# Expert gathers spread otherwise over the passes, modulation made during attention, and key norms by small matmuls, in a two-layer transformer kernel

## The chip, the cores and the metric

The kernel runs on one core of one Trainium2 chip. The metric is device time in microseconds, the median of several executions; less is better. Besides the median there is one profiled execution, and every duration quoted from the trace is from that one.

The core's engines each work through their own queue in order: PE (matmuls; PEld is its weight load), DVE (vector), ACT (activations and copies), POOL (general), and SP, which here only issues transfers. PE, ACT and POOL issue some transfers too.

## The reference, cut to what matters

Two layers run over 512 latent tokens and 256 context tokens of width 1024. Each layer does, for both kinds of token:

```python
# adaLN: six chunks of 1024 from silu(c) @ w_mod[l] + b_mod[l]; chunk 0 and 1 shift and scale the first norm,
# 2 gates the mixer's result, 3 and 4 shift and scale the second norm, 5 gates the experts' result
h = rms_norm(x, g) * (1 + scale) + shift
y = mixer(h)          # windowed attention, neighbourhood attention, RWKV-7, then one output projection
x = x + gate * y
h = rms_norm(x, g) * (1 + scale) + shift
x = x + gate * peer_ffn(h)

# in the RWKV-7 part, per head of 64 channels:
kk = kkh / maximum(sqrt(sum(kkh * kkh, axis=-1, keepdims=True)), 1e-12)

def peer_ffn(h, wq, sub_keys, u, v):      # 16384 experts, each one row of u and one of v
    s = scores of 8 heads against 2 x 128 sub-keys
    expert, best = 16 best of the sums, per head
    act = gelu(h . u[expert])
    return sum over the 128 chosen of softmax(best) * act * v[expert]
```

The context tokens leave no output of the last layer, so the second layer works out only the latent ones beyond its keys, values and states.

## The kernel before, in words

**Stages of a layer.** `project` makes the modulation and the norm, then the features of the RWKV part (`features`) and the queries, keys and values (`qkv`). `mix` runs the scan, the attention and the output projection. `peer` runs the norm, the scores, and the two dense passes over all experts, which the text calls U and V. In layer 0 the passes serve four tiles of 128 latent tokens, in layer 1 three.

**U pass.** 128 blocks of 128 experts. For each, a transfer brings two blocks' rows of `u` (1 MB), ACT casts `uH`, DVE makes the remainder `uL`, PE runs 8 x 3 matmuls into `pa`, and ACT writes `aw` (or the kept `ar`). Between blocks lie the pieces of the gates (`gates`): a piece spreads the 128 chosen gates of four tokens into a table over all experts, with two `oh` (L1231) and one `og` (L1234) of DVE, eight matmuls `pw` (L1239) and ACT's copy `W` (L1240). There are 128 pieces; after each eight `W`, which has one buffer, goes to memory (`wscr`, 2 MB). `GSPREAD` says over how many groups of four blocks the pieces are spread: 24 in layer 0. When the last piece is done, its pool is closed and a pool for later `ar` tiles (`late`) opens in the same memory; the first block that needs it is block 96.

**V pass.** The same 128 blocks, with `v` rows, `vH`, `vL`, the product `G` of gates and activations, its parts `GH` and `GL`, and 24 matmuls into `py` per block (18 in layer 1).

**Gathers.** The two context tiles (layer 0) and one latent tile (layer 1) take no dense pass. `class Gather` fetches for them the rows of `u` and `v` of one chosen expert per token with an indirect transfer of POOL (L1453, tile `row`, 128 tokens x 2048 numbers, 1.05 MB). Each pair of gathers then takes DVE two dot products (L1464), an activation, one multiply (L1467) and two multiply-adds (L1470). Layer 0 has 256 gathers, layer 1 has 128. They share their buffers `row` (`NROW` = 6) with the rows of `u` and `v`.

`NTICK` sets how many are issued: at each tick it adds a number to a balance, and each whole unit issues one gather at high priority. There is a tick at each of 5 steps of the scores, and after every second block: 24 in the first 12 groups of U, 40 in the rest of U, 64 in V. What is still left after V is issued by `flush()`. Then `ends` scales and adds the sums (L1399, L1400) and the `py` (L1409, L1410).

**Modulation.** `mod_unit` makes one chunk: 8 transfers of `wmod` (0.52 MB each), 32 matmuls, 4 of the bias, a copy `rmod`, two transfers out. In layer 0 chunks 0 and 1 stand ahead of the norm, and chunks 2 to 5 behind it at lower priority (`MOFF`). `mod_unit` is also called from `fill()`, which attention calls at places where PE may wait: there chunks 0 and 1 of layer 1 are made, in layer 0's context attention. Chunks 2 to 5 of layer 1 are made in layer 1's `project`.

**Key norms.** For each of four pairs of heads, a matmul with a block matrix of ones (`blk`, 128x128) sums the squares over 64 channels and repeats the sum in all of their rows: 128x768 numbers `rn`. ACT takes the root, DVE the maximum (L347) and the reciprocal (L348), POOL multiplies (L349). `rn` shares its buffer with ACT's `sg` (L360), by the tag "sg".

Order within an engine's queue comes from a scheduler that follows the written order and the priorities.

Of the kernel before, what the change touches and what calls it, by code (L numbers as in the profile page):

```python
# [8 lines left out]
F32 = mybir.dt.float32  # L9
# [4 lines left out]
AF = mybir.ActivationFunctionType  # L14
OP = mybir.AluOpType
AX = mybir.AxisListType
PSUM = bass.MemoryType.PSUM

P = 128
D = 1024  # L20
KC = 8
T = 768
NLAT = 512
NCTX = 256
NT = 6
# [9 lines left out]
LATER = 2000  # L35
NROW = 6
NQ = 2
MOFF = 500
GSPREAD = (24, 20)
LATE = (28, 28)  # L40
NM1 = 2
NMW = (6, 4)
NRAW = 4
TC0 = 6
NPSC, NPSL = 2, 4
# [9 lines left out]
NPRT = 4  # L55
NQKB = {"qs": 3, "kh": 3, "kl": 2}

NTICK = ((1, 1.0, 1.5, 2.4), (0, 0, 1.06, 1.06))
NFIRST = (12, 3)
FEATS = (12, 13, 4, 0, 5, 1, 6, 2, 7, 3, 14, 8, 9, 10, 11)  # L60
LAT = (0, 1, 2, 3)
# [5 lines left out]
class Kernel:  # L67
    nw = 0

    def __init__(self, ctx, tc, i, out, dbg):  # L70
        self.ctx, self.tc, self.nc, self.i, self.out, self.dbg = ctx, tc, tc.nc, i, out, dbg
        self.cp = ctx.enter_context(self.pool(name="cp", bufs=1))
        self.mods = list(range(NM1))

        self.xsb = {}
        self.consts()
        self.scratch()
# [150 lines left out]
    def project(self, l, st):  # L228
        tc, nc, i = self.tc, self.nc, self.i
        wc = l == 0  # L230
        cpl = self.colp[l]
        hp_ = st.enter_context(self.pool(name="hp", bufs=1))
        hH = hp_.tile([P, KC, T], F32R, name="hH")
        hL = hp_.tile([P, KC, T], F32R, name="hL")
        def mods(chunks):
            if s3.pools is None:
                s3.pools = [s3.enter_context(self.pool(name="mp", bufs=NMW[l], side="right")),
                            s3.enter_context(self.pool(name="mps", bufs=2, space=PSUM, side="right"))]
            self.mod(l, chunks, *s3.pools)

        def src(t):
            if l == 0:
                return i["x"][t * P:(t + 1) * P] if t < 4 else i["ctx"][(t - 4) * P:(t - 3) * P]
            return self.xp[t * P:(t + 1) * P]
        with ExitStack() as s3:
            s3.pools = None
            if l == 0:
                mods(range(2))
            with ExitStack() as s2:
                np_ = s2.enter_context(self.pool(name="np", bufs=2))  # L250
                nps = s2.enter_context(self.pool(name="nps", bufs=2, space=PSUM))
                mc = self.mcol[:, l, 0]
                for tiles in (CTX, LAT[:2], LAT[2:]):
                    self.norm_T(src, mc, hH, hL, tiles, np_, nps)
            if l:
                self.gat.close()
            with self.tc.high_priority(offset=-MOFF):
                mods(range(NM1 if l else 2, 6))
        ps = st.enter_context(self.pool(name="pps", bufs=2, space=PSUM))
        psn = st.enter_context(self.pool(name="psn", bufs=2, space=PSUM, side="right"))  # L260
        xp_ = st.enter_context(self.pool(name="xp", bufs=1, side="right"))
        win = i["w_in"][l].rearrange("(k p) n -> p k n", p=P)
        pre = st.enter_context(self.pool(name="pre", bufs=1)).tile([P, KC, 256], F32, name="pre")
        with ExitStack() as s2:
            b2 = s2.enter_context(self.pool(name="b2", bufs=2))
            pb = s2.enter_context(self.pool(name="pb", bufs=1))
            with self.tc.high_priority(offset=PREO):
                nc.sync.dma_start(pre, win[:, :, QKV0:QKV0 + 256])
            last = self.features(l, s2, win, hH, hL, ps, psn, xp_, b2, pb)
        with ExitStack() as s2:  # L270
            self.qkv(l, s2, win, hH, hL, ps, psn, pre)
        last()
# [9 lines left out]
    def features(self, l, st, win, hH, hL, ps, psn, xp_, b2, pb):  # L282

        nc, i = self.nc, self.i
        wc = l == 0
# [3 lines left out]
        gn = 6 if wc else 4  # L289
# [43 lines left out]
        for h in range(4):  # L333
# [4 lines left out]
            kk = b2.tile([P, T], F32, name="kk")  # L338
            nc.vector.tensor_scalar(kk, kf, cpl[:, KKC + h:KKC + h + 1], None, OP.mult)
            sq = b2.tile([P, T], F32, name="sq")  # L340
            nc.scalar.activation(sq, kk, AF.Square)
            rn = pb.tile([P, T], F32, name="rn", tag="sg")
            for (o, m) in segs:
                pz = ps.tile([P, m], F32, name="pf", tag=f"pf{m}")
                nc.tensor.matmul(pz, self.blk, sq[:, o:o + m], start=True, stop=True)
                nc.scalar.activation(rn[:, o:o + m], pz, AF.Sqrt)
            nc.vector.tensor_scalar(rn, rn, 1e-12, None, OP.max)  # L347
            nc.vector.reciprocal(rn, rn)  # L348
            nc.gpsimd.tensor_tensor(kk, kk, rn, OP.mult)  # L349
            nc.sync.dma_start(self.fm[2, :, h], kk)  # L350

            kAB, rate = [], []
            for d in range(2):
                sg = pb.tile([P, T], F32, name="sg", tag="sg")
                sga = b2.tile([P, T], F32, name="sga")
                r = slice(d * 64, d * 64 + 64)
                for (o, m) in segs:
                    pz = ps.tile([P, m], F32, name="pf", tag=f"pf{m}")
                    nc.tensor.matmul(pz, w2[r, h * P:(h + 1) * P], th[r, o:o + m], start=True, stop=True)
                    nc.scalar.activation(sg[:, o:o + m], pz, AF.Sigmoid, bias=cpl[:, W0 + 4 * d + h:W0 + 4 * d + h + 1])  # L360
                    pz = ps.tile([P, m], F32, name="pf", tag=f"pf{m}")
# [5 lines left out]
                for z in range(2):  # L367
# [4 lines left out]
                    c = b2.tile([P, NG, 65], F32, name="pr")  # L372
# [23 lines left out]
                                 bias=ka2[:, h:h + 1])  # L396
            nc.gpsimd.tensor_tensor(pd[:, :n], pd[:, :n], kf[:, :n], OP.mult)
            nc.gpsimd.tensor_tensor(pd[:, :n], pd[:, :n], rf[:, :n], OP.mult)
            pbn = psn.tile([P, gn, 2], F32, name="pn")
            for t in range(gn):  # L400
                nc.tensor.matmul(pbn[:, t], pd[:, t * P:(t + 1) * P], rkb[:, h], start=True, stop=True)
            nc.vector.tensor_copy(bon[:, :gn, 2 * h:2 * h + 2], pbn)
# [25 lines left out]
    def ngram(self, h, kAB, nmask, xp_, psn):  # L428


        nc = self.nc
        Nm = xp_.tile([P, 2, NG, 64], F32, name="Nm", bufs=2)
        for e in range(2):
            s = slice(e * 64, e * 64 + 64)
            for c0 in (0, 6):
                pn = psn.tile([P, 6, 64], F32, name="pn")
                for c in range(6):
                    for d in range(2):
                        nc.tensor.matmul(pn[64 * d:64 * d + 64, c], kAB[d][1][s, c0 + c], kAB[d][0][s, c0 + c],
                                         start=True, stop=True)  # L440
                nc.vector.tensor_tensor(Nm[:, e, c0:c0 + 6], pn, nmask.unsqueeze(1).to_broadcast([P, 6, 64]), OP.mult)
        for d in range(2):
            for j in range(2):
                r = 64 * d + 32 * j
                nc.sync.dma_start(self.nscr[h, d, j].rearrange("q s t -> s q t"),
                                  Nm[r:r + 32, :, :, 32 * j:32 * j + 32].rearrange("s e c t -> s (e c) t"))

        Nt = xp_.tile([112, 32, 32], F32, name="Nt", bufs=2)
        X = xp_.tile([112, 32, 32], F32, name="X", bufs=2)
        nc.sync.dma_start(Nt[0:48], self.nscr[h, 0].rearrange("j q s t -> (j q) s t"))  # L450
        nc.sync.dma_start(Nt[48:64], self.nscr[h, 0, 0, 0:16])
        nc.sync.dma_start(X[64:112], self.nscr[h, 1].rearrange("j q s t -> (j q) s t"))
        return Nm, Nt, X
# [110 lines left out]
    def attention(self, l, st):  # L564

        nc, i = self.nc, self.i
        wc = l == 0
        ap = st.enter_context(self.pool(name="ap", bufs=1))
        a2 = st.enter_context(self.pool(name="a2", bufs=2))
        psl = st.enter_context(self.pool(name="psl", bufs=NPSL, space=PSUM))  # L570
# [4 lines left out]
        mp = st.enter_context(self.pool(name="mp", bufs=2))  # L575

        def fill():
            if self.mods:
                self.mod_unit(1, self.mods.pop(0), mp, psl, "pl")

        def soft(parts, h, use_sink):

# [97 lines left out]
        if wc:  # L680
            heads_A(CTX, False)
            for c in range(2):
                o = a2.tile([P, NLAT], F32, name="o")[:, :NCTX]
                qs = [load_q(3 + c, z, NLAT, T) for z in range(2)]
                hd = [load_k(5 + c, z, NLAT) for z in range(2)]
                for a in range(2):
                    prTs = []
                    for z in range(2):
                        pl = psl.tile([P, 512], F32, name="pl")
# [15 lines left out]
        for c in range(2):  # L705
            o = a2.tile([P, NLAT], F32, name="o")
            qs = [load_q(3 + c, z, 0, NLAT) for z in range(2)]
            hd = [load_k(5 + c, z, 0) for z in range(2)]
            for j in range(4):
                prTs = []  # L710
                for z in range(2):
# [4 lines left out]
                    pl = psl.tile([P, 512], F32, name="pl")  # L716
# [704 lines left out]
class Gather:  # L1421
# [51 lines left out]
    def tick(self, z):  # L1473
        self.due += NTICK[self.l][z]
        while self.due >= 1 and self.todo:
            self.due -= 1
            with self.K.tc.high_priority(offset=100000):
                self.gather(*self.todo.pop(0))
# [75 lines left out]
```

## Time and the profile before

| | |
|---|---|
| median of 3 runs | 5100.41 us (5096.14 to 5110.7) |
| profiled execution | 5089.21 us, its span 5087.4 us |
| mean granted clock of PE | 0.906 of full speed |
| PE busy | 4438.3 us (87%) |
| DVE busy | 3738.1 us (73%) |
| ACT / POOL busy | 1731.5 us / 1338.2 us |
| moved by transfers | 1186.55 MB, mean 233 GB/s |

Of layer 0, modulation and norm take 0 to 73 us, features to 372, queries to 518, the scan to about 726, attention and output projections with the context's scores and choice to 1048, norm and scores to 1125, U to 2064, V to 2838, what follows V to 2885. Layer 1 starts there: norm to 2919, features to 3180, queries to 3346, scan, attention and output projection to 3692, scores to 3811, U to 4517, V to the end at 5087.

The rows below are read so: the busy time of an engine in a stretch says how near it is to being the bound there; the idle time before an instruction, in brackets, names what ended it; `x` is a count of instructions (a matmul of the modulation counts twice, so a chunk has 72).

### The profile page before, as it was taken

To read this page: it belongs to the slowest core of one execution; us is meant where nothing else is said; L and a number is where in the kernel's file an instruction comes from. 1 tells how busy PE (TensorE), PEld (TensorE's weight loads), DVE (VectorE), ACT (ScalarE), POOL (GpSimd) and SP (SyncE) were. 2 spreads that over 40 slices of the span, in tenths; PEclk is the share of its full clock that TensorE was granted. 3 is DMA by queue.
4 is the path that set the end of the run, shared out by engine and by line. 5 is a ranking of instruction groups with operands and counts; after the bars stand their busy time and mean duration, and the time that the engine had idled before them with its cause. 6 is when DMAs were issued, how large, how long until landed. Compare 5 with 4: busy or idle time off the path is not lost. (4 is left out here: it accounts for less than half of the span.)

```text
span 5087.4 us, 74067 instructions
## 1 busy us (share of the span) xinstructions
PE 4438.3 (87%) x27525; PEld 3679.1 (72%) x27525; DVE 3738.1 (73%) x7611; ACT 1731.5 (34%) x2881; POOL 1338.2 (26%) x1403
## 2 busy tenths in 40 slices
PE   7778797689999979898889596799698998988999
PEld 4558666567888867787777364687578997977887
DVE  3964658869967754798888867758589877556887
ACT  3433234333333322222222244324333443332333
POOL 0536632011111111232222235455011111112121
PEclk9779887799999989999999787779799998999999
DMA  7434665235777755899999942573424887567998
GB/s 273 134 104 125 190 203 177 90 128 197 250 260 283 281 217 214 305 372 371 367 364 368 349 162 87 131 204 111 157 100 170 305 296 278 215 236 256 342 357 299
DMA packets 573865, 1186.55 MB, mean 233 GB/s; under 512 B 63152, under 2 KB 376384, under 8 KB 520768
## 3 DMA queue, kind: packets, MB, share of 16 engines
q1 hardware_dynamic: 507072, 758.39, 44.8%
q0 software_dynamic: 61440, 418.41, 22.1%
q10 hardware_dynamic: 4992, 5.02, 0.3%
q8 instruction: 216, 3.54, 0.3%
q14 instruction: 145, 1.19, 0.1%
HBM read 1005.19 MB, written 176.50 MB: 232 GB/s over the span
## 5 line engine op out<-in xcount | busy, mean ns | idle before, releaser
L1453 POOL DMA_INDIRECT row<-in_uv,eidx x384 | 580.2, 1511 | 2465.2 <-DVE accc L1470 1369.1
L136 PE MATMUL pa<-hH,uL 128*128 128x512 f32 (+1 forms) x2048 | 757.9, 370 | 36.0 <-DVE uL L1313 35.9
L134 PE MATMUL pa<-hH,uH 128*128 128x512 f32 (+1 forms) x2048 | 754.5, 368 | 25.8 <-ACT ar L1317 21.6
L135 PE MATMUL pa<-hL,uH 128*128 128x512 f32 (+1 forms) x2048 | 752.4, 367 | 0.0
L135 PE MATMUL py<-vL,GH 128*128 128x512 f32 x1792 | 705.9, 394 | 26.6 <-DVE vL L1365 26.5
L136 PE MATMUL py<-vH,GL 128*128 128x512 f32 x1792 | 698.4, 391 | 0.0
L134 PE MATMUL py<-vH,GH 128*128 128x512 f32 x1792 | 625.2, 397 | 67.5 <-ACT vH L1363 44.1
L1464 DVE SCALAR_TENSOR_TENSOR row<-row,h2c 128x1024 f32<-128x1024 f32 x384 | 467.6, 1220 | 293.6 <-DMA row<-in_uv,eidx 293.3
L1470 DVE SCALAR_TENSOR_TENSOR accc<-row,dt,accc 128x1024 f32<-128x1024 f32 x384 | 491.6, 1280 | 5.4
L1311 ACT CAST uH<-row 128x1024 fp32r<-128x1024 f32 x256 | 268.5, 1050 | 653.7 <-PE pa L135 582.2
L136 PEld LDWEIGHTS pa<-hH,uL 128*128 128x128 f32 x2048 | 391.4, 191 | 84.8 <-DVE uL L1313 45.8
L134 PEld LDWEIGHTS py<-vH,GH 128*128 128x128 f32 x1792 | 340.9, 191 | 148.6 <-ACT vH L1363 53.4
L134 PEld LDWEIGHTS pa<-hH,uH 128*128 128x128 f32 x2048 | 391.6, 191 | 66.6 <-ACT ar L1317 22.2
L135 PEld LDWEIGHTS pa<-hL,uH 128*128 128x128 f32 x2048 | 390.9, 191 | 39.4
L135 PEld LDWEIGHTS py<-vL,GH 128*128 128x128 f32 x1792 | 341.3, 190 | 105.6 <-DVE vL L1365 34.5
L1313 DVE TENSOR_TENSOR uL<-row,uH 128x1024 fp32r<-128x1024 f32 x256 | 311.8, 1220 | 128.4 <-ACT uH L1311 127.5
L136 PEld LDWEIGHTS py<-vH,GL 128*128 128x128 f32 x1792 | 339.6, 189 | 70.7
L1370 ACT CAST GH<-G 128x512 fp32r<-128x512 f32 (+1 forms) x256 | 145.0, 567 | 637.7 <-PE py L135 414.9
L1365 DVE TENSOR_TENSOR vL<-row,vH 128x1024 fp32r<-128x1024 f32 x256 | 309.4, 1218 | 26.5 <-ACT vH L1363 26.5
L1363 ACT CAST vH<-row 128x1024 fp32r<-128x1024 f32 x256 | 262.5, 1043 | 41.7 <-DMA row<-in_uv 23.1
L1239 PE MATMUL pw<-og,oh 128*128 128x128 f16 x1792 | 237.7, 297 | 33.5 <-DVE og L1234 23.5
L1231 DVE TENSOR_TENSOR oh<-iota,ix 128x512 f16<-128x512 f16 x448 | 170.5, 419 | 104.8 <-PE pw L1239 103.9
(385 smaller groups left out, 8577.1 us busy)
## 6 DMA issues: line engine op xcount, KB each, us to landing
row<-in_uT SPq DMA_DIRECT2D x128, 1024.0 KB
row<-in_uv SPq DMA_DIRECT2D x128, 1024.0 KB
wscr<-W SPq DMA_DIRECT2D x28, 2048.0 KB
wmod<-in_w_mod SPq DMA_DIRECT2D x96, 512.0 KB
wt<-wscr SPq DMA_DIRECT2D x32, 1024.0 KB
row<-in_wq SPq DMA_DIRECT2D x24, 1024.0 KB
ascr<-aw SPq DMA_DIRECT2D x96, 256.0 KB
av<-ascr SPq DMA_DIRECT2D x48, 512.0 KB
```

The lines of the kernel that those rows point to most:

```text
L134: mm(out, lh, rh, start=first, stop=False)
L135: mm(out, lh, rl, start=False, stop=False)
L136: mm(out, ll, rh, start=False, stop=last)
L1231: nc.vector.tensor_tensor(oh[:, z], self.iota4, ix[:, z, tt].unsqueeze(1).to_broadcast([P, P, 4]), OP.is_equal)
L1239: nc.tensor.matmul(pw[:, q], oh[:, 1, :, q], og[:, z, :, q], start=z == 0, stop=z == 1)
L1311: nc.scalar.copy(uH, ur)
L1313: nc.vector.tensor_tensor(uL, ur, uH.bitcast(F32), OP.subtract)
L1363: nc.scalar.copy(vH, vr)
L1365: nc.vector.tensor_tensor(vL, vr, vH.bitcast(F32), OP.subtract)
L1453: self.K.nc.gpsimd.indirect_dma_start(out=r, out_offset=None, in_=self.K.i[f"uv{self.l}"], in_offset=bass.IndirectOffsetOnAxis(ap=self.idx ...
L1464: nc.vector.scalar_tensor_tensor(rows[z][:, 0:D], rows[z][:, 0:D], 1.0, self.h[:, a], OP.mult, OP.mult, accum_out=dt[:, z:z + 1])
L1470: nc.vector.scalar_tensor_tensor(acc, v, dt[:, z:z + 1], acc, OP.mult, OP.add)
```

## The change

**The table of ticks.** `NTICK` goes in layer 0 from 1 gather per tick in the scores, 1.0 in U's first 12 groups, 1.5 in the rest and 2.4 in V to 2, 1.8, 2.1 and 1.9; in layer 1 from 1.06 in U and V to 1.2 in U and 1.0 in V. Counted on DVE's queue, layer 0 had 88 gathers added up in the scores and U, 151 in V and 17 behind V; now it has 142, 114 and none.

**The modulation.** Only chunks 0 and 1 of layer 0 are made in `project`. Chunks 2 to 5 of layer 0 come in the first four fills of layer 0's attention, then all six of layer 1 in every third fill (`NMA`). The buffers for `wmod` in attention are two, as before there; in `project` of layer 0 there were six.

**The key norms.** Six small matmuls put the sums with tokens on partitions (128x12 for a pair of heads), where root, maximum and reciprocal are taken; twelve matmuls against the identity spread them back over the 64 channels into `pf`, and DVE multiplies from there in place of POOL. `rn` has its own buffer.

```diff
-MOFF = 500
-NM1 = 2
-NMW = (6, 4)
+NMA = 3
...
-NTICK = ((1, 1.0, 1.5, 2.4), (0, 0, 1.06, 1.06))
+NTICK = ((2, 1.8, 2.1, 1.9), (0, 0, 1.2, 1.0))
...
-        self.mods = list(range(NM1))
+        self.mods = [(0, c) for c in range(2, 6)] + [(1, c) for c in range(6)]
+        self.fills = 0
...
-            s3.pools = None
-            if l == 0:
-                mods(range(2))
+            if wc:
+                self.mod(l, range(2), s3.enter_context(self.pool(name="mp", bufs=6, side="right")),
+                         s3.enter_context(self.pool(name="mps", bufs=2, space=PSUM, side="right")))
...
-            with self.tc.high_priority(offset=-MOFF):
-                mods(range(NM1 if l else 2, 6))
...
-            rn = pb.tile([P, T], F32, name="rn", tag="sg")
+            pz = psn.tile([P, NT, 2], F32, name="pn", tag="pn")
+            for t in range(NT):
+                nc.tensor.matmul(pz[:, t], sq[:, t * P:(t + 1) * P], self.blk[:, 0::64], start=True, stop=True)
+            rn = b2.tile([P, NT, 2], F32, name="rn")
+            nc.scalar.activation(rn, pz, AF.Sqrt)
+            nc.vector.tensor_scalar(rn, rn, 1e-12, None, OP.max)
+            nc.vector.reciprocal(rn, rn)
             for (o, m) in segs:
                 pz = ps.tile([P, m], F32, name="pf", tag=f"pf{m}")
-                nc.tensor.matmul(pz, self.blk, sq[:, o:o + m], start=True, stop=True)
-                nc.scalar.activation(rn[:, o:o + m], pz, AF.Sqrt)
-            nc.vector.tensor_scalar(rn, rn, 1e-12, None, OP.max)
-            nc.vector.reciprocal(rn, rn)
-            nc.gpsimd.tensor_tensor(kk, kk, rn, OP.mult)
+                for a in range(0, m, P):
+                    for e in range(2):
+                        nc.tensor.matmul(pz[64 * e:64 * e + 64, a:a + P],
+                                         rn[:, (o + a) // P, e:e + 1].to_broadcast([P, 64]),
+                                         self.ident, start=True, stop=True)
+                nc.vector.tensor_tensor(kk[:, o:o + m], kk[:, o:o + m], pz, OP.mult)
...
         def fill():
-            if self.mods:
-                self.mod_unit(1, self.mods.pop(0), mp, psl, "pl")
+            self.fills += 1
+            if self.mods and (self.mods[0][0] == 0 or self.fills % NMA == 0):
+                self.mod_unit(*self.mods.pop(0), mp, psl, "pl")
```

In the rows of the changed kernel, line numbers before the attention are lower by up to nine, and those of U, V and the gathers are the same.

**ACT at the close of the gates in layer 0's U pass.** The rows are the queue of ACT between the last block that goes to memory and the first block of the `late` pool (`ar`). `W` is a piece of the gates, `dt` one pair of gathers, `uH` a block's cast. Before:

```order
L1240 ACTIVATE W<-pw 128x128x4 x2
L1311 CAST uH<-row 128x1024
L1240 ACTIVATE W<-pw 128x128x4 x4
L1466 ACTIVATE dt<-dt 128x2
L1240 ACTIVATE W<-pw 128x128x4 x9
L1466 ACTIVATE dt<-dt 128x2
L1240 ACTIVATE W<-pw 128x128x4
L1317 ACTIVATE ar_17363<-pa 128x512
```

The same place now, from the last block that goes to memory:

```order
L1466 ACTIVATE dt<-dt 128x2
L1240 ACTIVATE W<-pw 128x128x4 x5
L1466 ACTIVATE dt<-dt 128x2
L1240 ACTIVATE W<-pw 128x128x4 x2
L1466 ACTIVATE dt<-dt 128x2
L1240 ACTIVATE W<-pw 128x128x4 x6
L1466 ACTIVATE dt<-dt 128x2
L1240 ACTIVATE W<-pw 128x128x4 x3
L1466 ACTIVATE dt<-dt 128x2
L1240 ACTIVATE W<-pw 128x128x4 x16
L1317 ACTIVATE ar_17886<-pa 128x512
```

From the last `aw` on, 16 pieces stood there before and 34 stand there now (two of these, ahead of the rows, beside a `uH`), and five pairs of gathers stand in the rows in place of two.

**SP at the end of layer 0's context attention.** The rows are transfers that SP issues in order: `wmod` and `bmod` of the modulation, `qs`, `kh` and `kl` of the attention, `gr` the gate of the context's output projection, for which chunk 2 must be made, `TT` and `UV` of the scan. Before:

```order
L164 DMA wmod<-in_w_mod 128x1024 x4
L830 DMA TT_4536<-tscr 64x512 x2
L831 DMA UV_4538<-vt 64x512 x2
L628 DMA qs<-qkT 64x256 x4
L628 DMA kl<-qkT 64x256
L628 DMA kh<-qkT 64x256 x2
L628 DMA qs<-qkT 64x256
L622 DMA oT<-o 128x256
```

The same place now:

```order
L163 DMA wmod<-in_w_mod 128x1024 x6
L156 DMA bmod<-in_b_mod 4x256
L628 DMA kh<-qkT 64x256
L163 DMA wmod<-in_w_mod 128x1024 x2
L628 DMA qs<-qkT 64x256 x2
L628 DMA kl<-qkT 64x256
L628 DMA kh<-qkT 64x256
L163 DMA wmod<-in_w_mod 128x1024
L622 DMA oT<-o 128x256
L1057 DMA row<-od 128x512
L1068 DMA gr<-mscr 128x1024
L163 DMA wmod<-in_w_mod 128x1024 x5
```

Before, the `wmod` of the attention ended ahead of the loads of the context's second half; now they go on between them, eight more follow the five, and in all the queue has 80 of them in the attention where it had 16.

**DVE at the first pair of heads of layer 0.** `rn` are the norms, `kk` the keys, `raw` and `mcol` what stands between. Before:

```order
L347 TENSOR_SCALAR rn<-rn 128x768
L304 SCALAR_TENSOR_TENSOR raw<-pf,colp_71,raw 128x255
L348 RECIPROCAL rn<-rn 128x768
L339 TENSOR_SCALAR kk<-raw,colp_71 128x768
L179 COPY mcol<-pm 128x2x8
```

And now:

```order
L339 TENSOR_SCALAR rn<-rn 128x12
L295 SCALAR_TENSOR_TENSOR raw<-pf,colp_71,raw 128x255
L340 RECIPROCAL rn<-rn 128x12
L330 TENSOR_SCALAR kk<-raw,colp_71 128x768
L348 TENSOR_TENSOR kk<-kk,pf 128x512
L348 TENSOR_TENSOR kk<-kk,pf 128x256
```

Maximum and reciprocal run over 12 columns in place of 768, and two multiplies of 512 and 256 columns have come to DVE.

## Rows read from the trace of the kernel before

**Rows 1.** Busy time by stretch: us, then each engine, PE's clock, DMA share, GB/s.

```profile
0.00:73.00 73.00, 43.19 (x359) 14.32 (x359) 24.57 (x74) 26.92 (x51) 2.06 (x11) 0.88 0.99 356
100.00:160.00 60.00, 57.63 (x396) 38.97 (x395) 42.94 (x41) 30.84 (x42) 26.69 (x17) 0.97 0.55 194
180.00:280.00 100.00, 67.49 (x388) 49.77 (x386) 98.98 (x148) 41.37 (x56) 48.63 (x31) 0.72 0.29 95
634.00:995.00 361.00, 286.82 (x2487) 226.21 (x2487) 274.12 (x934) 143.76 (x318) 87.50 (x122) 0.80 0.49 154
1123.00:1370.00 247.00, 239.81 (x1131) 196.38 (x1130) 236.55 (x869) 88.56 (x128) 43.01 (x66) 0.99 0.59 205
1370.00:1812.00 442.00, 442.00 (x2313) 366.45 (x2313) 319.79 (x531) 158.10 (x250) 63.40 (x46) 1.00 0.76 278
1832.00:1874.00 42.00, 14.33 (x108) 11.31 (x105) 26.38 (x51) 8.87 (x17) 4.57 (x3) 0.54 0.62 233
2064.00:2838.00 774.00, 716.89 (x3070) 582.31 (x3071) 673.16 (x913) 211.77 (x328) 228.85 (x154) 0.98 0.99 361
2838.00:2885.00 47.00, 0.71 (x7) 0.28 (x9) 45.28 (x64) 1.64 (x7) 13.42 (x8) 0.54 0.91 343
2885.00:2919.00 34.00, 24.27 (x176) 9.18 (x176) 21.71 (x58) 22.89 (x46) 2.45 (x3) 0.70 1.00 358
4518.00:5087.00 569.00, 533.21 (x2304) 437.39 (x2304) 439.91 (x622) 191.81 (x288) 99.82 (x63) 0.97 0.89 310
```

**Rows 2.** PE's instructions one by one around the end of layer 0's V pass.

```profile
2836.68 0.39 PE L135 MATMUL py<-vL,GH 128*128 128x512 f32 x1
...
2838.26 0.39 PE L136 MATMUL py<-vH,GL 128*128 128x512 f32 x1
2884.94 1.08 PE L161 MATMUL pm<-wmod,cs 128*32 128x256 f32 x8 [46.29 <-DMA wmod<-in_w_mod]
```

**Rows 3.** Waits in V of layer 0 (2100 to 2826 us): total, times, longest.

```profile
PEld py L134 <- ACT vH L1363: 53.4, 22, 5.7
```

**Rows 4.** DVE's groups in U and V of layer 0, shapes apart.

```profile
L1470 DVE SCALAR_TENSOR_TENSOR accc<-row,dt,accc 128x1024 f32<-128x1024 f32 x239 | 306.0, 1280 | 3.5
L1464 DVE SCALAR_TENSOR_TENSOR row<-row,h2c 128x1024 f32<-128x1024 f32 x239 | 290.7, 1220 | 136.9 <-DMA row<-in_uv,eidx 136.6
L1231 DVE TENSOR_TENSOR oh<-iota,ix 128x512 f16<-128x512 f16 x256 | 97.6, 419 | 65.0 <-PE pw L1239 64.6 <-issue 0.2
L1234 DVE TENSOR_TENSOR og<-oh,g 128x1024 f16<-128x1024 f16 x128 | 86.0, 683 | 0.0
```

**Rows 5.** DVE's groups behind layer 0's V pass (2838 to 2885 us).

```profile
L1410 DVE TENSOR_TENSOR row<-row,yt 128x512 f32<-128x512 f32 x8 | 5.1, 681 | 0.0
```

**Rows 6.** ACT's first kept tile of the late pool, and the idle time ahead.

```profile
1874.04 1.09 ACT L1317 ACTIVATE ar<-pa 128x512 f32<-128x512 f32 x2 [12.76 <-DMA wscr<-W]
```

**Rows 7.** PE's work on the modulation (L161) by stretch.

```profile
0.00:73.00 73.00, 32.61 (x304) 8.17 (x304) 0.88 0.99 356
100.00:160.00 60.00, 10.46 (x128) 3.50 (x128) 0.97 0.55 194
634.00:726.00 92.00, 12.95 (x144) 3.18 (x144) 0.96 0.58 174
2919.00:3020.00 101.00, 15.36 (x160) 4.30 (x160) 0.89 0.57 193
```

**Rows 8.** Groups on ACT and DVE in layer 0's features (73 to 372 us).

```profile
L360 ACT ACTIVATE sg<-pf,colp 128x512 f32<-128x512 f32 x8 | 5.5, 686 | 20.7 <-POOL kk L349 20.6
L348 DVE RECIPROCAL rn<-rn 128x768 f32<-128x768 f32 x4 | 19.8, 4939 | 0.0
```

**Rows 9.** SP's queue one by one in layer 0's context attention.

```profile
663.00 7.80 SPq L164 DMA_DIRECT2D wmod<-in_w_mod  x2
680.89 6.94 SPq L164 DMA_DIRECT2D wmod<-in_w_mod  x4
```

**Rows 10.** Waits in the first part of layer 1's V pass (4518 to 4720 us).

```profile
DVE row L1464 <- DMA row<-in_uv,eidx: 55.8, 13, 9.5
```

More of the change, by code (lines that the diff above doesn't have):

```diff
@@ L234, in project @@
         hL = hp_.tile([P, KC, T], F32R, name="hL")
[L235 to L239, printed above, removed]
         def src(t):
@@ L398, in features @@
             nc.gpsimd.tensor_tensor(pd[:, :n], pd[:, :n], rf[:, :n], OP.mult)
-            pbn = psn.tile([P, gn, 2], F32, name="pn")
+            pbn = psn.tile([P, gn, 2], F32, name="pn", tag="pn")
             for t in range(gn):
@@ L435, in ngram @@
             for c0 in (0, 6):
-                pn = psn.tile([P, 6, 64], F32, name="pn")
+                pn = psn.tile([P, 6, 64], F32, name="pn", tag="pn")
                 for c in range(6):
```

## The prediction

> **What bounds the kernel now.** I read the busy times by stretch first, since the bound changes from stage to stage [rows 1]. At the start the transfers are the limit: DMA share 0.99 from 0 to 73 us. The features pass between PE (57.63 of 60 us from 100 on) and DVE (98.98 of 100 from 180 on, at a granted clock of 0.72). In attention and what surrounds it (634 to 995) no engine is full: PE 286.82 and DVE 274.12 of 361. The early part of U is held by two engines at once, DVE 236.55 and PE 239.81 of 247; its middle by PE alone (442 of 442, DVE 319.79). V of layer 0 is the odd stage: PE 716.89, DVE 673.16 of 774, and DMA share 0.99 at 361 GB/s.
>
> How far V is from PE's own limit comes from the instructions at its end: seven steps from 2836.68 to 2838.26 us, so 0.226 us per matmul [rows 2]. 24 x 128 matmuls make 3072 x 0.227 = 697 us. V took 774, so 77 us are lost, and the waits name late rows of `v`: 53.4 us of PE's weight loads stood for `vH` [rows 3]. Behind V, PE is idle for 46.29 us, until the next layer's `wmod` [rows 2], while DVE adds up the last gathers (45.28 of 47 us busy) [rows 1].
>
> The profiled execution took 5089.2 us, 11 less than the median; the sum is made against it, and 11 us are put on at the end. About 0.3%, 15 us, is what a measurement of this kernel can tell from no change.
>
> **Start and features of layer 0: -32 us.** In the first 73 us PE counts 304 matmul records of modulation [rows 7]; chunks 0 and 1 are 144, so 160 (2.2 chunks of 8 x 0.52 MB, 9.3 MB) are of chunks that now go elsewhere. At 356 GB/s these are 26 us. Bounds -4 and -18: the weights and tokens still have to come, and the norm behind `mcol` remains; I take -12. From 100 to 160, where PE is full, 10.46 us of PE's time go [rows 1, 7]; I take -8. Key norms: four reciprocals of 4.94 us on DVE [rows 8] and their maxima go; in their place come two multiplies per pair of heads. Those read PSUM as the sums behind V do, 0.68 us for 512 columns [rows 5], about 1.1 together, so some 4 us less per pair, 17 in all, part of it where DVE is full. ACT's `sg` also waited 20.7 us for POOL's `kk`, only because they share a buffer [rows 8]; that wait goes, but the matmul that feeds `sg` may be late next. The twelve new matmuls per pair are small and lie where PE has 30 of 100 us free [rows 1]. Between 0 and -50, near the DVE time in the full stretch: -12.
>
> **Attention of layer 0: +25 us.** 64 tiles of `wmod` come in. 144 records (16 tiles) took PE 12.95 us [rows 7], so 64 cost about 52 us. PE has 74 us idle in 634 to 995 [rows 1], but part of that is time in which DVE works on the choice and PE has nothing to be mixed with. If all fits, 0; if nothing fits, 52. SP's queue is the second cost: two buffers mean that it stands until PE has used a tile. Four tiles took 6.94 us, two took 7.80 [rows 9], 1.7 to 3.9 each. In SP's order 13 tiles now stand together at the end of the context's part, ahead of the latent `qs` and `kh` (23 us at 1.74 each), and chunk 2 is needed for `gr` of the context's projection. Taken as half of PE's 52; bounds 0 and +60.
>
> **Scores and U of layer 0: +48 us.** 54 more gathers are added up there. One costs DVE 1.22 + 1.28 = 2.50 us [rows 4], and I take 2.66 with the two short instructions that go with these. In the first 12 groups the ticks give 19 more (24 x 0.8), 51 us of DVE, where DVE has 10 us left [rows 1]. So the pieces of the gates slide: 18 more (16 to 34) stand in the bunch before the late pool. A piece takes DVE 2 x 0.419 + 0.683 = 1.52 us [rows 4], so 27 us leave the early part, and 51 - 27 - 10 = 14 remain, say +15. The bunch: 16 pieces kept PE from dense work for 42 us (busy 14.33) [rows 1], ended by `W` going out, ACT waiting 12.76 us [rows 6]. Without that wait a piece costs (43 - 13) / 16 = 1.9 us, with it 2.7; 18 more and 2 to 4 more gathers are +38 to +58, I take 50. In that stretch 108 matmuls, 8 to a piece, took PE 14.33 us [rows 1], about 1 us a piece, so PE has some 17 us less among the blocks before. So +33 there. The other 35 gathers fall where DVE has 122 of 442 us free [rows 1] and cost nothing; without that cover they would be 93 us. Bounds +15 and +80.
>
> **V of layer 0: -38 us.** 37 gathers fewer of 1.05 MB each. 774 us at 361 GB/s are 279 MB; 240 remain, 665 us, below PE's 697. So PE bounds, and the gain is at most 77. Layer 1's V is the model for what stays: 18 x 128 x 0.227 = 523 us of matmuls took 561 in all at DMA share 0.89 [rows 1], a loss of 38. Left with such a loss, V takes 736. Bounds 0 and -77.
>
> A rule stands beside this. The Trainium skill, "DMA: Bandwidth & Descriptors", section Bandwidth, gives 425 GB/s as measured for a 16 MB transfer, and warns there that HBM to SBUF is bound near 358 GB/s per core. By the first figure V's 279 MB would need 657 us (an estimate), PE would bound already and V would gain nothing; the row shows 361 GB/s at a share of 0.99, so the trace agrees with the second.
>
> **Behind V: -34 us.** No gather is left for the flush. What remains is `ends`: eight sums at 0.68 us for `py` [rows 5], the products ahead of them alike, about 11 us. 46.3 becomes 12. Bounds -25 and -38.
>
> **Project of layer 1: -31 us.** Chunks 2 to 5 no longer share the transfers from 2885 to 2919 (share 1.00) [rows 1], -9; 15.36 us of PE's modulation leave the next 101 us [rows 7], which PE bounds as in layer 0, -10; key norms as in layer 0, -12. Bounds 0 and -65.
>
> **Gathers of layer 1: -3 us, 15 either way.** Nine gathers go from V to U; early V waits 55.8 us on DVE for gathers [rows 10], which one gather per tick in place of 1.06 changes little.
>
> The sum: -32 + 25 + 48 - 38 - 34 - 31 - 3 = -65. 5089 - 65 = 5024 profiled, 5035 as a median.
>
> **The rivals.**
>
> *U hides its gathers.* DVE's 10 free us in the early part are a total of busy time; if the pieces' slide costs what it frees (PE's 17 us among the blocks, and the bunch overlapping the casts for the next blocks), U comes out at 0 instead of +48: -113, a median of 4987. For it speaks that PE and DVE are idle in the bunch for two thirds and a third of the time; against it that the bunch is serial through the one buffer of `W`.
>
> *V is not shortened.* V's loss may come from the sharing of six `row` buffers, not from bytes: each gather holds a buffer until DVE is through, and U will now hold them likewise. Then V keeps its 774, the rest stands: -65 + 38 = -27, and with U at its upper half (+63), -12: a median of 5088. For it speaks that `vH` waits for few long gaps (22 waits, 5.7 at most) [rows 3]; against it the share of 0.99 over the whole stage.
>
> *SP and PE are held by the modulation in attention: slower.* A fill's matmuls stand in PE's queue, and everything behind them waits for their tile. At 3.75 us per tile (the slow row) [rows 9], 64 tiles are 240 us; less the 74 us of idle PE [rows 1] that is +166 in place of +25: +76, a median of 5176. It decides from about +105 us in that stage, where the other terms (-90) are used up and 15 remain. For it speaks that PE stands in order and the buffers are two; against it that tiles back to back took 1.74 us and that the scheduler puts other matmuls between most of them.
>
> That the change doesn't do what it says is excluded for the gathers and the chunks by the counts in the queues. It is open only for the price.
>
> **How the numbers follow.** The forecast, with its sum between -30 and -95, has 0.55; U hiding its gathers 0.17; V not shortened 0.16; the slower rival 0.12. Predicted is 5035. Of the forecast about 0.04 lies within 15 us of 5100; of V not shortened about half. Faster by over 0.3%: 0.51 + 0.17 + 0.09 = 0.77; within: 0.04 + 0.07 + 0.01 = 0.12; slower: 0.11. The range 4970 to 5105 holds the forecast, most of the first rival and most of the second; the slower one lies outside, as does a U that hides everything with V at PE's limit. The forecast's own range is 5005 to 5070.
>
> **What the profile after would show.** Right: V of layer 0 near 736 us with DMA share clearly under 0.99; PE idle behind V about 12 us; no more than 0.5 us for any reciprocal of the key norms and no `sg` waiting for `kk`; PE's gap before the late pool between 80 and 100 us; the first feature matmul near 61 us in place of 73. Wrong: a gap before the late pool of 45 us or below (first rival); V at 760 or more (second); from scan's end to the context's choice longer by over 100 us with PE waiting on `wmod` (third). The prediction would also fail if the late context path (chunks 2 to 4) delayed the choice of experts, so that gathers are missing at U's first ticks and pile up again behind V.

## The result, and the profile after

The changed kernel takes 5242.09 us (median of 4 runs, 5238.32 to 5246.49) where the kernel before takes 5101.0 (median of 4). The ratio is 1.0274, interval 1.0257 to 1.0292: slower by 141 us where 65 us less were forecast. The forecast's range ended at 5105. The profiled execution has a span of 5244.7 us at a granted clock of 0.889, against 5087.4 at 0.906, so the two traces differ by 157 us. Differences below are between medians measured side by side, unless a ratio is named.

Where these 157 us arise is read from the start of the first or last matmul of a stage in both traces; U and V are taken from DVE's first `uL` and `vL`, and attention ends with its last score matmul:

| stage | before, us | after, less before | forecast |
|---|---|---|---|
| start to first feature matmul, layer 0 | 73.0 | -4 | -12 |
| features and queries, to the scan's first matmul | 448.3 | +22 | -20 |
| scan to its last matmul | 203.5 | +25 | in attention |
| from there to the end of attention | 239.2 | +140 | +25 |
| output projection, norm and scores | 161.3 | +3 | in U |
| U with the step to V | 938.5 | +42 | +48 |
| V | 774.6 | -28 | -38 |
| behind V, to layer 1's first feature matmul | 80.8 | -45 | -43 |
| layer 1, from there to U | 823.1 | -8 | -22 |
| U and V of layer 1 | 1336.9 | +9 | -3 |

Some 10 us of the scan are probably chance of the one profiled execution of before, which was 11 us under its median: in all the runs below, also where its code is the same, the scan takes 5 to 25 us more.

Busy times by stretch after, columns as in [rows 1]: the start, the attention with the context's scores and choice, a piece of it, U's early part, its middle, V, and what lies behind V.

```profile
0.00:69.00 69.00, 35.65 (x196) 11.77 (x196) 23.79 (x71) 26.37 (x48) 3.38 (x12) 1.00 0.61 215
661.00:1102.00 441.00, 338.38 (x2914) 232.39 (x2913) 255.02 (x842) 116.31 (x256) 88.60 (x125) 0.73 0.64 201
780.00:800.00 20.00, 8.39 (x64) 1.61 (x64) 0.00 (x0) 0.37 (x1) 0.00 (x0) 0.50 0.68 202
1312.00:1545.00 233.00, 220.22 (x995) 177.80 (x995) 223.97 (x783) 74.47 (x112) 60.65 (x75) 0.99 0.71 245
1545.00:1983.00 438.00, 433.27 (x2227) 359.42 (x2226) 366.26 (x637) 154.08 (x247) 95.05 (x65) 1.00 0.86 322
2292.00:3038.00 746.00, 707.49 (x3069) 577.90 (x3070) 599.80 (x803) 206.61 (x311) 168.12 (x116) 0.99 0.93 330
3038.00:3075.00 37.00, 15.86 (x53) 7.52 (x52) 27.57 (x68) 22.83 (x45) 3.95 (x4) 0.54 0.41 121
```

V went in the direction of the forecast: DMA share 0.93 where it was 0.99, DVE 600 us busy where it was 673, PE 707 of 746. Behind V, PE idles 9.5 us in place of 46.29 [rows 2]: the first row is V's last matmul, the second a transpose of the next norm.

```profile
3038.51 0.39 PE L135 MATMUL py<-vH,GL 128*128 128x512 f32 x1
3048.40 1.35 PE L209 MATMUL pt<-c_ident,xn 128*128 128x128 f32 x4 [9.50 <-DVE xn L203]
```

The attention is the loss. For 20 us from 780 on DVE does nothing at all, ACT and POOL next to nothing, and PE only multiplies `wmod` and its bias. PE's rows of that stretch (start, duration, and in brackets the idle time ahead and what ended it):

```profile
788.02 1.08 PE L160 MATMUL pl<-wmod,cs 128*32 128x256 f32 x8 [2.24 <-DMA wmod<-in_w_mod]
790.68 1.08 PE L160 MATMUL pl<-wmod,cs 128*32 128x256 f32 x8 [1.58 <-DMA wmod<-in_w_mod]
793.56 1.08 PE L160 MATMUL pl<-wmod,cs 128*32 128x256 f32 x8 [1.80 <-DMA wmod<-in_w_mod]
796.23 1.08 PE L160 MATMUL pl<-wmod,cs 128*32 128x256 f32 x8 [1.58 <-DMA wmod<-in_w_mod]
```

One tile every 2.7 us, with everything behind it in PE's queue held. SP's queue at the same place, a duration being how long SP was taken up:

```profile
769.73 14.42 SPq L163 DMA_DIRECT2D wmod<-in_w_mod  x5
785.84 20.27 SPq L163 DMA_DIRECT2D wmod<-in_w_mod  x8
```

Thirteen tiles take SP 34.7 us, and the attention's own loads (`qs`, `kh`, `kl`) stand behind them. From the list of waits from 650 to 1312 us (total, times, longest), the weight loads and the matmuls of the modulation, which overlap, and POOL's casts of `qs`, which waited 33.5 us for these loads before:

```profile
POOL qb L718 <- DMA qs<-qkT: 77.8, 2, 74.3
PEld pl L160 <- DMA wmod<-in_w_mod: 77.2, 40, 6.5
PE pl L160 <- DMA wmod<-in_w_mod: 59.7, 34, 5.6
```

PE's waits for tiles are thus far less than the 140 us. SP's queue shows another way to the same loss. These are the last loads of `qs` in the attention, before and after:

```profile
885.90 1.09 SPq L628 DMA_DIRECT2D qs<-qkT  x2
1110.18 1.09 SPq L628 DMA_DIRECT2D qs<-qkT  x2
```

Counted from the end of the scan they are issued 161 us on before and 342 us on now, and the last score matmul comes at 239 and 379 us. The context's scores end only 51 us later than before, the other 89 us arise behind them, in what is left of the latent attention.

### The profile page after: what moved, and what is told of

It reads as the page before. It is cut to its first block, busy times and chain, and to the rows that moved or that the text cites. A ratio compares the mean times of both kernels' runs of the same rounds, so it can differ in the third digit from the quotient of the medians.

```text
span 5244.7 us, 74591 instructions
## 1 busy us (share of the span) xinstructions
PE 4520.1 (86%) x27781; PEld 3736.6 (71%) x27781; DVE 3706.0 (71%) x7627; ACT 1732.0 (33%) x2880; POOL 1327.5 (25%) x1395
## 5 line engine op out<-in xcount | busy, mean ns | idle before, releaser
L1453 POOL DMA_INDIRECT row<-in_uv,eidx x384 | 563.8, 1468 | 2474.6 <-DVE accc L1470 1377.2
L133 PE MATMUL py<-vH,GH 128*128 128x512 f32 x1792 | 659.9, 393 | 31.6 <-ACT GH L1370 21.3
L1239 PEld LDWEIGHTS <-oh 128*128 128x128 f16 x1792 | 190.2, 119 | 116.3 <-DVE og L1234 63.6
```

Source lines behind the costliest of these rows:

```text
L133: mm(out, lh, rh, start=first, stop=False)
L1239: nc.tensor.matmul(pw[:, q], oh[:, 1, :, q], og[:, z, :, q], start=z == 0, stop=z == 1)
L1453: self.K.nc.gpsimd.indirect_dma_start(out=r, out_offset=None, in_=self.K.i[f"uv{self.l}"], in_offset=bass.IndirectOffsetOnAxis(ap=self.idx ...
```

## The experiments

### The three parts apart

**The ticks alone.**

```diff
-NTICK = ((1, 1.0, 1.5, 2.4), (0, 0, 1.06, 1.06))
+NTICK = ((2, 1.8, 2.1, 1.9), (0, 0, 1.2, 1.0))
```

> Only the table of ticks is changed, modulation and key norms as before. Theory (U pays, V and its end give back, each at about the size seen in the whole change: U +42, V -28, behind V -35, layer 1 +9): -12 us, ratio 0.997 to 0.999. Rival (the longer U of the whole change comes from the late start of the gathers there, not from the ticks): U unchanged, -55 us, ratio 0.99. Second rival (ticks alone are the loss): over +40 us.

Measured: ratio 0.988 (0.9862 to 0.9898), 5047.81 us, -57. That is the second theory's number, but by luck: what it named did not show, since U is 26 us longer (output projection and scores 13 more), V 28 shorter, behind V 40 shorter. Those add up to -30, more than the first theory's -12. What neither had is layer 1 ahead of its U, 34 us shorter, though its ticks only begin in U. (The two traces differ by 33 us and not by 57, as the profiled execution of before lies under its median and that of this run over it.)

**The key norms alone**: the hunk of the diff that takes the sums to 128x12, on the kernel before.

> Only the key norms are changed. Theory (the small matmuls stand in PE's order between others and make PE wait for ACT and DVE, so the features get longer): features of layer 0 +20 us, of layer 1 +10, total +30 us, ratio 1.006. Rival (the features got longer because the modulation's matmuls no longer fill PE there): -20 us, ratio 0.996, no `sg` waiting for `kk`.

Measured: ratio 1.0141 (1.012 to 1.0161), 5173.79 us, +69. The direction is the first theory's; the size is double. The features and queries of layer 0 are 34 us longer. The rows of PE for the fourth pair of heads, in order of time (L447 the Gram products of the pair before, L409 its bonus, L345 the new sums, L354 the spreading; rows of `pj` between them are left out):

```profile
298.84 1.54 PE L447 MATMUL pn<-kA,kB 64*64 64x64 f32 x24 [7.74 <-DVE Nm L449]
300.66 1.54 PE L447 MATMUL pn<-kA,kB 64*64 64x64 f32 x24
302.48 2.72 PE L409 MATMUL pn<-rkb,sq 128*128 128x2 f32 x12
305.59 2.72 PE L345 MATMUL pn<-c_blk,sq 128*128 128x2 f32 x12
309.90 2.83 PE L354 MATMUL pf<-c_ident,rn 128*64 128x128 f32 x24
```

ACT had the squares ready long before:

```profile
258.69 0.84 ACT L341 ACTIVATE sq<-kk 128x768 f32<-128x768 f32 x1
```

The squares end at 259.5 and their sums start at 305.6, 46 us later. All three products are named `pn` and take turns in its two buffers, so the new sums stand in the queue behind the Gram products of the pair before, which themselves wait for DVE and, in rows not shown, for POOL.

**The modulation alone**: the rest of the diff, ticks and norms as before.

> Only the modulation is moved; ticks and key norms as before. Theory (this is the loss of the whole change): scan's start to U's first block +150 to +170 us, start and layer 1's norm -15 to -25, total +135 us, ratio 1.026. Rival (the loss needs the late context path and the ticks together): under +60 us, ratio under 1.012.

Measured: ratio 1.0204 (1.0176 to 1.0233), 5201.28 us, +97 where the theory had +135 and the rival under 60. Attention is 137 us longer behind the scan, as in the whole change (+140); layer 1 ahead of U is 28 us shorter. The loss needs neither the ticks nor the norms.

### What in the modulation costs

**Four buffers.**

```diff
-        mp = st.enter_context(self.pool(name="mp", bufs=2))
+        mp = st.enter_context(self.pool(name="mp", bufs=4))
```

> As the run with only the modulation moved, but with four buffers for `wmod` in attention where there are two. Theory A (two buffers: SP cannot issue the next tile before PE has used one, so each tile pays its whole way): at least 60 us less than with two, total +40 to +75. Theory B (PE's order: the matmuls stand ahead of others and take PE's time at the lower clock, and the context path waits for chunks 2 to 4): within 20 us of the run with two.

Measured: ratio 1.0071 (1.0044 to 1.0098), 5134.85 us, +30: 66 us less by two more buffers, theory A, though the total lies under its range of 40 to 75. Attention is 49 us longer than before in place of 137. The waits of PE for tiles, 640 to 1150 us:

```profile
PEld pl L160 <- DMA wmod<-in_w_mod: 11.7, 12, 2.7
PE pl L160 <- DMA wmod<-in_w_mod: 7.9, 8, 2.3
```

With two buffers the same rows are these:

```profile
PEld pl L160 <- DMA wmod<-in_w_mod: 68.7, 37, 4.3
PE pl L160 <- DMA wmod<-in_w_mod: 53.0, 34, 5.3
```

These waits are 45 to 57 us shorter, some of that in the scan. With that goes a higher clock. Over the attention behind the scan, these are the busy times with two buffers:

```profile
728.00:1104.00 376.00, 274.92 (x1731) 185.73 (x1729) 226.94 (x822) 109.05 (x246) 45.54 (x74) 0.68 0.55 178
```

And with four:

```profile
728.00:1016.00 288.00, 227.57 (x1607) 164.33 (x1601) 215.03 (x804) 109.18 (x245) 45.39 (x74) 0.79 0.62 207
```

Of the 88 us between the two stretches, 41 are idle time of PE. Another 23 are matmuls of the modulation, 480 records (55.8 us) in place of 360 (33.1 us), as more of them are done during the scan with four buffers. The other matmuls are the same, 1251 and 1247, and are busy for 219 us in place of 194, at a granted clock of 0.68 in place of 0.79. Before the change the clock was 0.77 here, from 725 to 964 us.

The last `qs` of the attention, which SP issued 342 us behind the scan in the whole change and 338 here with two buffers, is issued at 229 with four.

**One tile per chunk.**

```diff
-            w = pool.tile([P, 1024], F32, name="wmod")
-            nc.sync.dma_start(w, src[:, k])
+            if k == 0 or tag == "pm":
+                w = pool.tile([P, 1024], F32, name="wmod")
+                nc.sync.dma_start(w, src[:, k])
```

> As the run with only the modulation moved, two buffers, but a chunk made in attention loads only its first tile of `wmod` and uses it for all eight steps, so the result is another and 70 of 80 transfers are left out; PE's work is the same. Theory A (the tiles' way through two buffers is the loss): at least 75 us less than the +97 of that run, total +20 or below. Theory B (PE's work in its order at the lower clock, and the context path behind it): +60 or more.

Measured: ratio 0.9983 (0.9969 to 0.9997), 5089.41 us. With the same matmuls and 70 transfers fewer the loss is gone, theory A; PE's work in its order is at most a small part (attention +13 us behind the scan), and the last `qs` is issued 175 us behind the scan. It also shows the ceiling: even if the tiles cost nothing, moving the modulation gains some 7 us here. The run takes away both what PE waits for and what stands in SP's queue, so it doesn't tell which of the two queues held the attention; loading `wmod` from another engine's queue would, and was not tried.

**Layer 1's chunks only.**

```diff
-        self.mods = list(range(NM1))
+        self.mods = list(range(6))
+        self.fills = 0
...
-                mods(range(NM1 if l else 2, 6))
+                mods(range(6 if l else 2, 6))
...
-            if self.mods:
+            self.fills += 1
+            if self.mods and self.fills % 3 == 0:
```

> Chunks 2 to 5 of layer 0 stay in its project as before; all six of layer 1 are made in layer 0's attention, every third fill, two buffers. Theory C (the loss is that the context path waits for layer 0's chunks 2 to 4): +0 to +25 us. Theory A (each tile costs its way, wherever it stands; 32 more tiles than before in place of 64): attention half as much longer, total about +50.

Measured: ratio 1.01 (1.0077 to 1.0123), 5147.47 us, +51: what theory A gave. Attention is 76 us longer for half as many tiles. That the context path waited for its own chunks is not needed for the loss.

### The mended parts, and together

**The norms' sums in a buffer of `pf`.**

```diff
-            pz = psn.tile([P, NT, 2], F32, name="pn", tag="pn")
+            pz = ps.tile([P, 256], F32, name="pf", tag="pf256")[:, :2 * NT].rearrange("p (t z) -> p t z", z=2)
```

> Only the key norms are changed, and their 128x12 sums go to a buffer of `pf` in place of one of the two that the sums share with the Gram products `pn`. Theory 1 (a pair's norm has to wait for the Gram products of the pair before to leave the shared `pn` buffers): the +69 us of the run with the norms alone shrink to at most +15. Theory 2 (PE's own added work, some 5.5 us per pair at the lower clock, and the longer chain through PE, ACT and DVE in PE's order): +45 to +70 as before.

Measured: ratio 0.9944 (0.9925 to 0.9962), 5069.79 us: -27 in place of +69, with the same matmuls. Theory 1, beyond its own number (at most +15). The fourth pair's rows, where the sums now stand ahead of most of the Gram products:

```profile
236.44 1.40 PE L345 MATMUL pf<-c_blk,sq 128*128 128x2 f32 x12
245.59 2.82 PE L447 MATMUL pn<-kA,kB 64*64 64x64 f32 x44 [7.75 <-POOL d L377]
252.94 2.83 PE L354 MATMUL pf<-c_ident,rn 128*64 128x128 f32 x24 [4.53 <-DVE rn L349]
```

The sums start at 236 where they started at 306, 5 us behind their squares (230.52 to 231.35).

**The whole change with four buffers.**

> The whole change, but four buffers for `wmod` in attention. Theory A: as with the modulation alone, 67 us less than the whole change with two, +74 to the kernel before, ratio 1.0145. Rival (in the whole change other waits take over, since the parts add up to 109 and the whole is 141): under 40 us less, ratio over 1.019.

Measured: ratio 1.0127 (1.0098 to 1.0156), 5154.5 us: some 75 us less than the whole change, by the two ratios. Theory A.

**The whole change with both mends.**

> The whole change with both mends, four buffers for `wmod` in attention and the norms' sums in a `pf` buffer. If the ring of `pn` cost the whole change what it cost the norms alone (95 us): +65 - 95 = -30, ratio 0.994. If the parts add up without loss: -57 - 27 + 30 = -54. Rival (the loss of the norms was hidden behind that of the modulation): above 0.

Measured: ratio 1.0056 (1.0032 to 1.0079), 5135.71 us, +28. The second expectation, that the parts add up, and the first both fail; the rival has the sign. The mend gives 36 us by the ratios, where alone it gave 100. Against the whole change with four buffers, features and queries of layer 0 come down from +21 to +3 us and its scan from +25 to +17, but attention behind the scan goes from +48 to +60. In layer 1 the scan comes down from +47 to -1, yet the features and queries ahead of it (-42 becomes -19) and the end of attention (-18 becomes +2) take back all but 7 us. These stages don't show the 36 us: the profiled execution of this run was its slowest (5152.45), and the two traces have the same span within 1 us. Why attention takes 12 us more there stays open.

**Ticks and mended norms, modulation as before.**

> The new table of ticks and the key norms with their sums in a `pf` buffer; modulation as before. If the two gains (57 and 27 us) add up: -84 us, ratio 0.9835. Rival (both fill the same idle time): -45 to -60.

Measured: ratio 0.9905 (0.9875 to 0.9935), 5054.1 us, -53: the gains don't add up. U is 42 us longer where it was 26 with the ticks alone: PE's dense work stops for 95.7 us at the late pool (35 pieces of the gates) where it stopped for 79.5 (32 pieces). That the shorter features shift the order is likely, but not shown.

**Fewer gathers ahead of the late pool, more behind it.**

```diff
-NTICK = ((2, 1.8, 2.1, 1.9), (0, 0, 1.2, 1.0))
+NTICK = ((2, 1.2, 1.6, 1.9, 3.5), (0, 0, 1.2, 1.0, 1.2))
...
-                        gat.tick(1 if g < NFIRST[l] else 2)
+                        gat.tick(4 if late else 1 if g < NFIRST[l] else 2)
```

> As the run before it, but fewer gathers in U ahead of the late pool (1.2 and 1.6 per tick in place of 1.8 and 2.1) and more behind it (3.5), V as there. The queue of ACT has 24 pieces of the gates between the last block that goes to memory and the late pool, where the run before it has 32. Theory (U pays for the pieces that slide into this bunch, 2.7 us each): 20 us less than that run, -105, ratio 0.9795. Rival (the blocks behind take the gathers no more cheaply, since their buffers are shared): within 8 us of that run.

Measured: ratio 0.9825 (0.9793 to 0.9856), 5012.58 us, -95: 41 us less than the run before it. U is 20 us longer than before (for 42), and V 46 shorter (for 23). The stretch at the late pool, then V:

```profile
1835.00:1908.00 73.00, 28.41 (x205) 22.11 (x205) 67.37 (x123) 18.68 (x36) 19.62 (x12) 0.54 0.87 335
2088.00:2817.00 729.00, 702.66 (x3072) 577.38 (x3072) 606.05 (x811) 210.39 (x314) 171.51 (x115) 0.99 0.97 346
```

The stop is 72 us, with 25 pieces. The theory's 20 us came in U (22), the rival falls. What it did not name is V, which now runs near PE's limit (703 of 729) at a DMA share of 0.97. V has no fewer gathers for it: by their start times in the traces 149 before the change, 114 in the run before this one, 116 here. So the gain in V comes from elsewhere, and stays open. This is the fastest of all kernels here.

**Layer 0's row of ticks alone.**

```diff
-NTICK = ((1, 1.0, 1.5, 2.4), (0, 0, 1.06, 1.06))
+NTICK = ((2, 1.8, 2.1, 1.9), (0, 0, 1.06, 1.06))
```

> Layer 0's row of the new table of ticks alone, layer 1's as before. Theory (layer 1's part before U is shorter in the run with both rows because nothing is left behind V and the order of its instructions came out otherwise): that stays, -50 to -62 us. Rival (layer 1's own row brings it): -15 to -35.

Measured: ratio 0.991 (0.9883 to 0.9936), 5057.89 us, -50. The theory's side: layer 1 ahead of its U stays 31 us shorter. Nothing of layer 1's code is changed ahead of its U, so another order of the same instructions is the likely cause, but no run shows it. Of the 31 us, 25 lie in features and queries. The time from the scan's end to the end of attention in layer 1 shrinks too (by 1 to 44 us in every run but the whole change with both mends, +2), but in most of these runs the scan ahead of it is longer by as much as 49 us, so part of that only moves the border between the two.

## Why the prediction was wrong

**The step that failed** is the attention of layer 0, +25 us with an upper bound of 60. From the scan's first matmul to U it became 168 us longer. The step took PE's time for the matmuls as the main cost and halved it; the tile's way was the cost. The price was in the rows: SP took 7.80 us for two tiles at one place and 6.94 for four at another [rows 9], and the forecast used 1.74 us, the cheaper. After, it is 2.5 to 2.9 us of SP each, and 2.7 us between PE's steps. By that price 64 tiles would be 173 us, close to the 168, but this is partly luck, since not all tiles paid it: by the runs a tile more cost 2.1 us of attention (137 us for 64) and 2.4 (76 for 32). Two buffers are the cause as far as edits can show it: four take 66 us off with all else alike, and leaving the transfers out takes off all of the loss. This is the slower rival, which the prediction priced at +166 us in that stage (with 3.75 us a tile, where the row gives 3.9) and gave 0.12. Its sign, over 100 us by the context's choice with PE waiting for `wmod`, came only in part: counted from the scan's end, the context's choice ends 63 us later, and PE's waits are 60 to 77 us; most of the rest came in the latent attention, whose loads stood in SP's queue behind the tiles. The prediction named these loads, and priced the 13 tiles ahead of them at 23 us, where they took 34.7. It argued against the rival that the scheduler puts other matmuls between; PE's rows show up to 11 tiles in a row (from 777.68 us), and the order showed 13 together in SP's queue.

The move also brought less elsewhere than the prediction gave it. In the run with the modulation alone the start is 5 us shorter, the features and queries of layer 0 are 3 and the step to layer 1's features 3, where -12, -8 and -9 were forecast; only layer 1 ahead of its U has 28 where 10 were forecast.

**The second failure** is the key norms. The count of instructions was right, and the forecast of -12 and -12 us is about what the norms give with a buffer of their own, -27; but by stage this is 8 in layer 0 and 21 in layer 1 ahead of U, and no run tells which of the terms brings it. What the prediction left out is the two buffers of `pn`, which tie the sums of one pair of heads to the Gram products of the pair before. The diff gives the tile that name, so this could have been read. The cover that was named, idle PE, was there and of no use: the sums were not allowed to run in it. In the whole change, going by the two runs with four buffers, the shared buffers cost 18 us in features and queries of layer 0, 8 in its scan and 7 in layer 1 ahead of U.

**What held.** Scores and U, +48, came as +42 with 3 more in output projection, norm and scores (with the ticks alone 26 and 13). The stop at the late pool was forecast at 80 to 100 us and is 98.7, with 32 pieces in it. It lies between these two rows of PE, the last dense matmul ahead of it and the first behind:

```profile
2005.81 0.39 PE L135 MATMUL pa<-hH,uL 128*128 128x512 f32 x1
2104.48 0.80 PE L133 MATMUL pa<-hH,uH 128*128 128x512 f32 x1 [7.70 <-ACT ar L1317]
```

The rival in which U hides its gathers falls. V's -38 came as -28, and with the ticks placed otherwise as -46, so the rival in which V is not shortened falls. Whether it was bytes that bound V, at 361 GB/s before (374 from 2193 to 2322 us), is not shown: fewer gathers also hold fewer of the shared `row` buffers. What is left of V's loss after the change looks more like the buffers, since 26 of the 39 us in which PE is not busy lie in its first 249 us, at a share of 0.84, while SP's rows of `v` wait for `accc`, that is for gathers to give their buffers back. First the busy times of that stretch, then the longest wait of SP's queue in it (total, times, longest):

```profile
2292.00:2541.00 249.00, 223.28 (x946) 180.21 (x947) 185.00 (x255) 63.40 (x97) 57.39 (x39) 0.97 0.84 287
SPq L1360 <- DVE accc L1470: 83.2, 11, 13.9
```

Behind V and in layer 1's first norm -45 came where -34 and -9 were forecast. The start gave -4 for -12, the lower bound: the transfers' share fell from 0.99 to 0.61, and the first step of the norm on ACT began at 49.2 us where it began at 49.5.

**What was missing** in the sum: layer 1 ahead of its U, which is 31 to 35 us shorter in the runs with new ticks and the old modulation, where nothing was forecast. It makes the parts alone look better than they are together: ticks, modulation and norms alone are -57, +97 and +69, which is 109, and the whole is 141. In layer 1 ahead of U the three alone are -34, -28 and +16, which is -46, and the whole is -8. This is told by the stages of the traces; its cause stays open, and no run tries it by itself.

## What to carry to other kernels

When a stream of loads is moved next to other work, the number of its buffers sets its price: take the slow row of a tile's way with that many buffers, not the fastest, and multiply by all tiles that the engine's queue holds in a row (here that, less the idle time, gave +166 us where the stage took 168, the closeness being partly luck). Look also at what stands behind these loads in the queue that issues them. When a small product is given a shared buffer, read which older products the queue must finish first; idle time of the engine is no cover for work that is not allowed to start. And where DVE is full, added work there moves whatever the program can still put off, here the gates, to the next point where all of it must be done: look for that point and add the work behind it.

## What was not expected of the hardware

Standing still for tiles costs more than the standing. In the run with the modulation alone the granted clock over the attention is 0.68 with two buffers and 0.79 with four, and the same 1250 matmuls beside the modulation are busy for 219 and 194 us. In the whole change, in the 20 us in which PE only waits and multiplies `wmod`, the clock is 0.50, the lower of its two levels. Eight matmul records of `wmod` take 1.08 us there; at the start of the kernel before, at 62.10 us and a clock of 1.00, they took 0.64.
